# A hybrid streaming-encoder trunk: other ranks and places for weight sums, background loads, two norms and the first dots

## The chip, the cores and the metric

The kernel runs on one core of one Trainium2 chip. A core has five engines, each with its own instruction stream: TensorE (PE, matmuls; PEld is its weight load), VectorE (DVE), ScalarE (ACT), GpSimd (POOL) and SyncE (SP). An engine runs its instructions in the order in which they were put into its stream; it waits at an instruction until what that needs is there, and everything behind it waits too. Transfers are issued by SP, ACT and POOL and run on the core's DMA engines. The metric is the device time of one execution in microseconds (us), the median of several runs.

## The reference

Two layers over a sequence of 512 positions with 16 meta tokens ahead of it (T = 528), model width 2048. The even layer projects the normed input into a convolution group and an attention group, gates each, and projects the sum back; the odd layer is a gated linear recurrence with 16 heads.

```python
def even_mixer(hn, ...):
    glu_v, glu_g, gate_a, q, c, gate_b, qi, ki, wi = split_last(hn @ w_in, EVEN_SPLITS)
    u = glu_v * jax.nn.sigmoid(glu_g)
    u = conv(u, conv_w) + conv_b                       # causal, depthwise, width 31
    a_out = silu(layer_norm(u, ln_g, ln_b)) * silu(gate_a)
    c = rms_norm(c, kv_g)                              # the latent
    ...                                                # index dots, top-k mask, attention over c
    b_out = einsum(o_lat, w_uv) * silu(gate_b)
    return concatenate([a_out, b_out]) @ w_out

def odd_mixer(hn, ...):
    q, fz, i, g = split_last(hn @ w_in, ...)
    o = hgrn2_chunkwise(silu(q), log_f(fz), k(fz), i)
    o = rms_norm(o) * norm_g * silu(g)
    return o @ w_out

for layer in range(2):
    h = h + mixer[layer](rms_norm(h, norm_gain[layer]))
return rms_norm(h, final_norm_gain)[:, 16:]
```

## The kernel before

Everything lies transposed: features on the 128 partitions, positions along the free axis. A **stripe** (`stripe`) is 128 output features against all 2048 inputs. Its weights come as one 1 MB load `w`; `square_sum` (L192, ScalarE, output `junk`) adds up their squares, an all-reduce on POOL (L144, `tot`) sums over the partitions, and from that VectorE makes a power-of-two scale (`u` L148, `sc` L199, `inv` L201). Then each half is split into two float16 tiles: `wh` by ScalarE (L208) and `wl` by VectorE (L209). TensorE takes three matmuls for each k tile (wh by xh, wh by xl, wl by xh; L268 to L270), 96 for a stripe of two halves of 264 columns. `split` (L317, L318) makes the pairs xh and xl of the input in the same way.

The order of each engine's stream is made by a planner when the program is built: every instruction has a rank (`band`: WGT 5 above EVAC 4, SIDE 3, CONV 2), and the planner takes the ready one of the highest rank, by its own estimate of times. `behind(name)` puts what follows after the instruction that was noted as `queued[name]` on its stream. `at(us, job)` puts a side job behind a given point of a running count (`clock`) of the stripes' matmul time. The work runs in stages:

- **Input and first stripes.** x is loaded, normed and split into the 16 tiles X0 (L419, L317). Stripes `kw` and `c` come first; from `c` the latent is normed (`csq`, `rc`, L494). The bias table is built from `onehot` by four loads and small matmuls (L485) and written to DRAM (`bdram`).
- **EVEN stage.** A list gives the order of stripes: `g` convolution gates (`glu`, followed by 31 convolution steps on VectorE, L617 and L619, tile `z`), `s` index stripes (`scores`), `k` the top-k masks (`select`, L588 to L591), `h` attention heads (`head`, `attend`), `n` the layer norm. A `scores` stripe evacuates its two halves (L559, L560), exchanges them between partition halves by two transfers on POOL (L562, `uh<-pa` or `ul<-pa`), and its `dots` (L572, L573) follow as side jobs, 7 us later by the running count; ScalarE and VectorE add them into the masks (L575, L576). In a head, POOL loads a row block of biases (`L<-bdram`, L644), adds the mask to it by a transfer (`L<-mask`, L646), then come scores (L654), softmax (L656 to L663), transposes (L683, L686) and values (L697).
- **Background loads.** `later` holds 48 transfers on POOL's queue that form sums of output weights in DRAM (`es`, L368). `send` issues a few at a time: one or two at the places called `aside`, two in each `scores`, and one behind each mask of heads 6 and 7. `foresee` loads weights of later stages and squares them.
- **Layer norm** of the convolution, as two side jobs, `mean` and `spread` (Ln L335, Exp L336), rank CONV.
- **Mixing and first output.** Gates `gate_a`, then eight output **pairs** p, each of seven products of 24 matmuls (L979): `pair_begin` loads weights and, from p = 2, squares four of them; `pair_corner` and `pair_rest` do the products and the adds (`add`, L986). Within `pair_rest(0)` pair 2 is begun.
- **Odd layer.** 48 stripes and 16 recurrences (`rec_head`, L1150 to L1156 in its levels), then 16 gate stripes. Beside them the 16 weight blocks of the last output are loaded (`gw`) and squared, one in each gate stripe (two `junk` of 1024 columns), for `pair_scales`, which makes the scales of the last eight pairs. Then come these pairs (`pair_stripes`) and the final norm.

Of the kernel before, what the change touches and what calls it, by code (L numbers as in the profile page):

```python
# [74 lines left out]
def trunk_kernel(ctx: ExitStack, tc: tile.TileContext, x: bass.AP, w: bass.AP, wukv: bass.AP,  # L75
# [139 lines left out]
    def load(s, back, keep=None, known=None):  # L215

        w32 = load_raw(s)
        if known is None:
            ss = wpool.tile([128, 1], F32, name="ss", bufs=4)
            with behind("S"):  # L220
                square_sum(w32, ss)
            total = wpool.tile([128, 1], F32, name="tot", bufs=4) if keep is None else keep
            all_sum(total, ss)
            known = scales(total, back)
# [26 lines left out]
    def stripe(s, X, back, wide=True, order=(0, 1), ring=None, keep=None, known=None):  # L251
# [6 lines left out]
        with band(WGT):  # L258
            hi, lo, inv = load(s, back, keep, known)
# [54 lines left out]
    def split(pair, src, scale):  # L314

        xh, xl = pair[:, 0, :], pair[:, 1, :]
        S.activation(xh, src, AF.Identity, scale=scale)  # L317
# [98 lines left out]
    with band(WGT):  # L416
        for k in range(KT):
            t = et([128, T], F32, "sq", 3)
            V.tensor_tensor(t, xin[k], rstd0, op=OP.mult)  # L419
            X0.append(split(xp.tile([128, 2, T], F16, name="x", bufs=KT), t, gains[:, 0, k:k + 1]))  # L420

# [68 lines left out]
    with band(SIDE):  # L490
        rc = et([128, T], F32, "acc", 2)
        rstd_from(mean_bcast(ones_c, csq, None), rc, eps_r, et([128, T], F32, "sq", 3))
        for j in range(2):
            V.scalar_tensor_tensor(cn[j], cn[j], col(V_KV + j), rc, op0=OP.mult, op1=OP.mult)  # L494
            CX.append(split_rounded(E, cn[j]))
# [52 lines left out]
    def scores(j):  # L548
        ps, inv = stripe(S_QI + j, X0, back0, wide=False)
        catch_up()  # L550
        send(later, 2)
# [5 lines left out]
        with band(EVAC):  # L557
            for q, hi, lw, hf, other in ((qa, qa, ql, lo, up), (qb, ql, qb, up, lo)):
# [3 lines left out]
                G.dma_start(q[other], ql[hf])  # L562
# [16 lines left out]
        for t in range(NB):  # L579
            for hh in range(2):  # L580
                at(clock[0] + 7.0 + 1.2 * (2 * t + hh), lambda t=t, hh=hh: dots(t, hh))
# [17 lines left out]
    def glu(i):  # L599
        ps, inv = stripe(S_GLU + 2 * i, X0, half0)  # L600
        g = et([128, T], F32, "gt", 3)
        with band(EVAC):
            for p, sl in ps:
                S.activation(g[:, sl], p, AF.Tanh, scale=inv)
        aside(i > 2)
        ps, inv = stripe(S_GLU + 2 * i + 1, X0, back0)
        aside(i > 2)
# [29 lines left out]
    def attend(h, qh, gb, Kh, Vt):  # L637
# [4 lines left out]
        def softmax(t, nq, q0, W):  # L642
            e = et([128, T], F32, "L", 5)
            queued[f"B{h}"] = G.dma_start(e[:nq, :W], bias_rows(h, q0, nq, 0, W))  # L644
            if t < NB:
                queued["B"] = G.dma_start(e[:, :W], M[t], accum_op=OP.add)  # L646
                if h >= 6:
                    send(later, 1, "B")
# [69 lines left out]
    def head(h):  # L718
# [7 lines left out]
        aside(True)  # L726
        ps, inv = stripe(S_GQ + 2 * h + 1, X0, back0)
        catch_up()
        aside(True)
# [35 lines left out]
    def aside(late):  # L765

        send(later, 1 if late else 2)
# [5 lines left out]
    def layer_norm():  # L773

        def mean():
            with band(CONV):
# [5 lines left out]
                for p, sl in mean_bcast(ones_a, [zs], None):  # L782
                    S.activation(mu[:, sl], p, AF.Copy)
# [11 lines left out]
        def spread(vs_):  # L795
            nonlocal rz
            with band(CONV):
# [187 lines left out]
    def add(dst, p, scale):  # L985
        V.scalar_tensor_tensor(dst, p, scale, dst, op0=OP.mult, op1=OP.add)  # L986
# [63 lines left out]
    def pair_rest(p, raw, scale, banks, following):  # L1050
# [12 lines left out]
        for bank_, wt, xs, first, dst, scl in ((b, s2, u2, True, ha[:, t2], ninv), (a, w12, x21, False, ha[:, t1], inv),  # L1063
# [3 lines left out]
            with band(EVAC):  # L1067
                add(dst, bank_, scl)
                if wt is s4:
                    first_square(2 * p)  # L1070
# [299 lines left out]
    osc, oinv, oninv = oq[:, 2, :].bitcast(I32), oq[:, 3, :].bitcast(I32), oq[:, 4, :]  # L1370

    def pair_scales(c):

        sl = slice(4 * c, 4 * c + 4)
        with band(EVAC):
# [5 lines left out]
            V.tensor_scalar(osc[:, sl], u, -1.0, 204 * EXP, op0=OP.mult, op1=OP.add)  # L1381
            V.tensor_scalar(oinv[:, sl], u, oback, None, op0=OP.add)
            V.tensor_scalar(oninv[:, sl], oinv[:, sl].bitcast(F32), -1.0, None, op0=OP.mult)

    ahead = 1
    early_load(S_OO)
    for i in range(8):
        for h in (i, 8 + i):
# [20 lines left out]
    osc, oinv = osc.bitcast(F32), oinv.bitcast(F32)  # L1409
# [72 lines left out]
    for n in range(0, KT - 2, 2):  # L1482
        pair_stripes(n)
    with band(WGT):
# [127 lines left out]
```

## Time and profile before

| | us |
|---|---|
| median of 3 runs (lowest to highest) | 1842.26 (1841.38 to 1843.06) |
| the profiled execution | 1841.84 |
| its span in the trace | 1839.7 |
| VectorE busy | 1394.8 (76%) |
| ScalarE busy | 1237.3 (67%) |
| POOL busy | 225.3 (12%) |
| weight splits on ScalarE (`wh<-w,sc` L208) | 214 of 1143 ns |
| weight squares on ScalarE (`junk<-w` L192) | 114, mean 1674 ns |
| es loads on POOL's queue | 48 from the weights (512 KB, median 7.9 from issue to landing) and 16 from es |

How to read it: the page has one execution of the program. A row of a timeline gives the start, the duration, the engine, the line, the operation, out<-in with the shape, and in brackets how long the engine was idle before it and what ended that idle time. A row of the waits gives the waiting engine and line, the one waited for, us in total, how many times, and the longest. A row of the windows gives a stretch, its length, the busy time of each engine, the granted TensorE clock as a share of full speed, the DMA share and GB/s.

### The profile page before, as it was taken

Reading aid. Unit: us, or ns where it says so; the run is one execution under the profiler, and the core shown is the slowest. Engines: PE = TensorE matmul, PEld = TensorE weight load, DVE = VectorE, ACT = ScalarE, POOL = GpSimd, SP = SyncE. Lnnn points to the kernel's source line nnn. Section 1 sums busy time; section 2 is a strip of 40 time slices with the busy share of each in tenths; the row PEclk is TensorE's granted clock in tenths of the full one; section 3 lists DMA queues with packets and bytes.
Section 4 is the critical chain, followed back from the end, with each engine's and each line's share of the span. In section 5 each row is a group of like instructions: output and inputs, shape, how many; then the busy total and the mean of one; then the engine's idle time right before and its main releaser. Section 6 shows DMA issues by size and latency. Waiting matters only on the chain.

```text
span 1839.7 us, 36579 instructions
## 1 busy us (share of the span) xinstructions
PE 1802.2 (98%) x14678; PEld 1393.2 (76%) x14678; DVE 1394.8 (76%) x2836; ACT 1237.3 (67%) x2035; POOL 225.3 (12%) x399
## 2 busy tenths in 40 slices
PE   9989999999999899999999999999999999999997
PEld 6666588888888788888777777877777765446886
DVE  7599979998875577777787777777777776757774
ACT  4755675667666666675687777778787777865563
POOL 1312211132222200000110100101010000001000
PEclk9999999999999999999999999999999999999998
DMA  5856666668565745774665555455654445556553
GB/s 202 266 159 195 177 178 188 187 181 227 165 197 133 191 130 188 255 249 163 200 195 138 177 161 174 160 157 152 170 165 146 138 143 178 183 197 238 197 187 109
DMA packets 81339, 330.97 MB, mean 180 GB/s; under 512 B 10288, under 2 KB 17752, under 8 KB 65840
## 3 DMA queue, kind: packets, MB, share of 16 engines
q1 hardware_dynamic: 40592, 190.51, 29.4%
q0 software_dynamic: 25600, 87.64, 20.0%
q10 hardware_dynamic: 14976, 50.47, 8.3%
q8 instruction: 115, 1.88, 0.4%
q14 instruction: 56, 0.46, 0.1%
HBM read 309.75 MB, written 73.87 MB: 209 GB/s over the span
## 4 chain that ended last, share of the span: by engine, by line
PE 67%; DVE 6%; ACT 4%; issue 3%; DMA 2%; POOL 1%; ACTq 0%; SPq 0%; DVEq 0%; POOLq 0%
PE mps L268 15%; PE mps L269 15%; PE mps L270 15%; PE mps L979 13%; DVE z L619 2%; DMA w<-in_w_dram 1%; ACT junk L192 1%; DVE wl L209 1%; PE po L697 1%; PE s L979 1%; ACT wh L208 1%; PE s L1155 1%; PE s L1154 1%; PE s L1156 1%; PE po L1277 1%
## 5 line engine op out<-in xcount | busy, mean ns | idle before, releaser
L268 PE MATMUL mps<-x,wh 128*128 128x264 f16 (+1 forms) x2880 | 864.9, 300 | 2.8 <-ACT x L317 2.8
L270 PE MATMUL mps<-x,wl 128*128 128x264 f16 (+1 forms) x2880 | 864.6, 300 | 0.0
L269 PE MATMUL mps<-x,wh 128*128 128x264 f16 (+1 forms) x2880 | 864.3, 300 | 0.2
L268 PEld LDWEIGHTS <-wh 128*128 128x128 f16 x2880 | 283.1, 98 | 110.0 <-issue 7.9
L269 PEld LDWEIGHTS <-wh 128*128 128x128 f16 x2880 | 283.1, 98 | 108.0 <-issue 3.3
L270 PEld LDWEIGHTS <-wl 128*128 128x128 f16 x2880 | 283.0, 98 | 106.6 <-issue 2.9
L208 ACT ACTIVATE wh<-w,sc 128x1024 f16<-128x1024 f32 x214 | 243.3, 1143 | 136.3 <-PE mps L269 81.3
L209 DVE SCALAR_TENSOR_TENSOR wl<-w,sc,wh 128x1024 f16<-128x1024 f32 x214 | 272.6, 1279 | 57.5 <-ACT wh L208 55.9
L192 ACT ACTIVATE junk<-w 128x2048 bf16<-128x2048 f32 (+2 forms) x114 | 190.8, 1674 | 26.2 <-DMA w<-in_w_dram 23.3
L979 PEld LDWEIGHTS <-wh 128*128 128x128 f16 x1808 | 177.4, 98 | 28.6 <-issue 2.2
L619 DVE SCALAR_TENSOR_TENSOR z<-u,vec,z 128x528 f32<-128x528 f32 x240 | 179.4, 760 | 1.9
L144 POOL PARTITION_ALL_REDUCE tot<-ss x78 | 42.4, 543 | 688.2 <-ACT junk L192 688.2
L979 PEld LDWEIGHTS <-wl 128*128 128x128 f16 x904 | 88.7, 98 | 13.3 <-DVE wl L209 1.2
L208 ACT ACTIVATE wh<-w,oq 128x1024 f16<-128x1024 f32 x53 | 60.6, 1148 | 54.6 <-PE mps L979 46.3
L209 DVE SCALAR_TENSOR_TENSOR wl<-w,oq,wh 128x1024 f16<-128x1024 f32 x53 | 67.8, 1283 | 28.1 <-ACT wh L208 28.0
L979 PE MATMUL mps<-on,wh 128*128 128x256 f16 x464 | 78.1, 273 | 0.1
L192 ACT ACTIVATE junk<-gw 128x1024 bf16<-128x1024 f32 x64 | 66.9, 1045 | 2.5 <-DMA gw<-in_w_dram 2.2
L1151 DVE SCALAR_TENSOR_TENSOR qlm<-q,qhm 128x256 f16<-128x256 f32 x128 | 52.5, 421 | 20.8 <-ACT qhm L1150 20.8
L1150 ACT ACTIVATE qhm<-q 128x256 f16<-128x256 f32 x128 | 51.1, 411 | 21.7 <-DVE q L1252 19.3
L979 PE MATMUL mps<-on,wl 128*128 128x256 f16 x232 | 63.2, 273 | 0.0
L209 DVE SCALAR_TENSOR_TENSOR wl<-w,gsc,wh 128x1024 f16<-128x1024 f32 x32 | 41.0, 1281 | 28.4 <-ACT wh L208 28.2
L209 DVE SCALAR_TENSOR_TENSOR wl<-w,gaq,wh 128x1024 f16<-128x1024 f32 x30 | 38.5, 1283 | 22.3 <-ACT wh L208 22.1
(544 smaller groups left out, 3282.3 us busy)
## 6 DMA issues: line engine op xcount, KB each, us to landing
w<-in_w_dram SPq DMA_DIRECT2D x116, 1024.0 KB, 5.0
gw<-in_w_dram ACTq DMA_DIRECT2D x64, 512.0 KB, 6.4
es<-in_w_dram POOLq DMA_DIRECT2D x48, 512.0 KB, 7.9
w<-in_w_dram SPq DMA_DIRECT2D x47, 512.0 KB, 4.5
os<-in_w_dram POOLq DMA_DIRECT2D x42, 512.0 KB, 7.9
w<-es SPq DMA_DIRECT2D x32, 512.0 KB, 5.1
w<-os SPq DMA_DIRECT2D x28, 512.0 KB, 4.5
pa<-in_w_dram ACTq DMA_DIRECT2D x24, 512.0 KB, 4.0
```

Of the source, the lines that this page charges most:

```text
L144: queued["G"] = G.partition_all_reduce(out, src, channels=128, reduce_op=op or bass_isa.ReduceOp.add)
L192: S.activation(junk[:, :src.shape[-1]], src, AF.Square, accum_out=ss)
L208: queued["S"] = S.activation(hi, src, AF.Identity, scale=sc)
L209: V.scalar_tensor_tensor(lo, src, sc, hi, op0=OP.mult, op1=OP.subtract)
L268: P.matmul(o, hi[half][:, ws], xh[:, sl], start=n == 0 and k == 0, stop=False)
L269: P.matmul(o, hi[half][:, ws], xl[:, sl], start=False, stop=False)
L270: mm = P.matmul(o, lo[half][:, ws], xh[:, sl], start=False, stop=n == 1 and k == 7)
L619: V.scalar_tensor_tensor(z, u[:, j:j + T], col(V_CW + i * CW + j), z, op0=OP.mult, op1=OP.add)
L697: P.matmul(state["o"][:, 128 * t:128 * (t + 1)], Vt[:, j, :], pt[:, j, :], start=j == 0, stop=j == t + 1)
L979: P.matmul(p, wt[:, sl], xt, start=start and k == i == 0, stop=stop and k == 7 and i == 2, skip_group_check=stop and not start and resume)
L1150: S.activation(hi, src, AF.Copy, scale=scale)
L1151: V.scalar_tensor_tensor(lo, src, scale, hi, op0=OP.mult, op1=OP.subtract)
```

## The change

It moves work and leaves what is computed as it was.

- The square sum of the first index stripe's weights is put behind the split of the last input tile (`early="X0"`).
- The latent norm becomes a side job at 6.0 of the running count, of rank EVAC, with one table of functions loaded behind the first convolution gate's tanh.
- The dots of the first index stripe come 14 instead of 7 us later; no background load is sent in that stripe, and in the others they are sent behind the exchange. The first convolution gate sends none, the others two at each `aside`, the heads one, the masks of heads 6 and 7 none.
- The layer norm's mean matmuls, their evacuation and the Ln and Exp get rank EVAC.
- Pair 2 is begun in `pair_rest(1)`, so that on ScalarE all splits of pair 1 stand ahead of the four square sums of pair 2; the weights of the stripe behind the last pair, or of any stripe behind a noted `V`, come behind the add of the last `s4`.
- Gate stripes 0 and 8 do no weight squares; the last two blocks are squared behind the first two pairs of the last output.

```diff
@@ load, stripe, split
-    def load(s, back, keep=None, known=None):
+    def load(s, back, keep=None, known=None, early="S"):
...
-            with behind("S"):
+            with behind("S"), behind(early):
                 square_sum(w32, ss)
...
-        with band(WGT):
-            hi, lo, inv = load(s, back, keep, known)
+        with band(WGT), behind("V"):
+            hi, lo, inv = load(s, back, keep, known, early)
+        queued.pop("V", None)
...
-        S.activation(xh, src, AF.Identity, scale=scale)
+        queued["A"] = S.activation(xh, src, AF.Identity, scale=scale)
...
             X0.append(split(xp.tile([128, 2, T], F16, name="x", bufs=KT), t, gains[:, 0, k:k + 1]))
+        queued["X0"] = queued["A"]
@@ the latent norm
-    with band(SIDE):
-        rc = et([128, T], F32, "acc", 2)
-        rstd_from(mean_bcast(ones_c, csq, None), rc, eps_r, et([128, T], F32, "sq", 3))
...
+    def latent():
+        with band(EVAC):
+            rc = et([128, T], F32, "acc", 2)
+            pieces = mean_bcast(ones_c, csq, None)
+            with behind("T"):
+                ready = S.preload_act_table_set("natural_log_exp_and_others")
+            with tc.issue_after(ready.ins):
+                rstd_from(pieces, rc, eps_r, et([128, T], F32, "sq", 3))
...
+    at(6.0, latent)
@@ scores
-        ps, inv = stripe(S_QI + j, X0, back0, wide=False)
+        ps, inv = stripe(S_QI + j, X0, back0, wide=False, early="X0" if j == 0 else "S")
         catch_up()
-        send(later, 2)
...
-                G.dma_start(q[other], ql[hf])
+                queued["X"] = G.dma_start(q[other], ql[hf])
+        if j:
+            send(later, 2, "X")
...
-                at(clock[0] + 7.0 + 1.2 * (2 * t + hh), lambda t=t, hh=hh: dots(t, hh))
+                at(clock[0] + (7.0 if j else 14.0) + 1.2 * (2 * t + hh), lambda t=t, hh=hh: dots(t, hh))
@@ glu, softmax, head, aside
-                S.activation(g[:, sl], p, AF.Tanh, scale=inv)
-        aside(i > 2)
+                queued["T"] = S.activation(g[:, sl], p, AF.Tanh, scale=inv)
+        aside(2 if i else 0, i > 2)
...
                 queued["B"] = G.dma_start(e[:, :W], M[t], accum_op=OP.add)
-                if h >= 6:
-                    send(later, 1, "B")
...
-        aside(True)
+        aside(1, True)
...
-    def aside(late):
+    def aside(n, late):
 
-        send(later, 1 if late else 2)
+        send(later, n)
         if late:
             foresee()
@@ layer_norm
-                for p, sl in mean_bcast(ones_a, [zs], None):
-                    S.activation(mu[:, sl], p, AF.Copy)
+                with band(EVAC):
+                    for p, sl in mean_bcast(ones_a, [zs], None):
+                        S.activation(mu[:, sl], p, AF.Copy)
...
         def spread(vs_):
             nonlocal rz
-            with band(CONV):
+            with band(EVAC):
@@ pair_rest
-                add(dst, bank_, scl)
+                last = add(dst, bank_, scl)
                 if wt is s4:
+                    queued["V"] = last
                     first_square(2 * p)
...
-        nxt = pair_rest(p, *begun[p], banks[p], p + 2 if p == 0 else p + 1 if p > 1 else 8)
+        nxt = pair_rest(p, *begun[p], banks[p], p + 1 if p else 8)
@@ the gates and the last output
-    ahead = 1
+    ahead = 0
+
+    def early_square():
+
+        nonlocal ahead
+        for c in range(2):
+            square_sum(raws.pop(0), oss[:, ahead, c:c + 1])
+        ahead += 1
+        if ahead < KT:
+            early_load(S_OO + ahead)
+        if ahead % 8 == 0:
+            pair_scales(ahead // 16)
+
...
             with band(CONV), behind("S"):
-                if raws:
-                    for c in range(2):
-                        square_sum(raws.pop(0), oss[:, ahead - 1, c:c + 1])
-                if ahead < KT:
-                    early_load(S_OO + ahead)
-                ahead += 1
-            if ahead in (9, 17):
-                pair_scales(ahead // 16)
+                if h not in (0, 8) or i:
+                    early_square()
...
         pair_stripes(n)
+        if ahead < KT:
+            with band(CONV), behind("S"):
+                early_square()
```

Line numbers of the changed kernel are one higher from L268 on, and about 10 to 13 higher from L494 on. Three places in the streams:

On ScalarE, in the first stripes, before (`junk,ss` are square sums, `x<-sq,gains` the input tiles):

```order
L469 ACTIVATE sq<-gb 128x528
L208 ACTIVATE wh<-w_743,sc 128x1024 x2
L469 ACTIVATE sq<-gb 128x528
L192 ACTIVATE junk,ss<-w_901 128x2048
L317 ACTIVATE x<-sq,gains 128x528
L208 ACTIVATE wh<-w_901,sc 128x1024 x2
```

and now:

```order
L471 ACTIVATE sq<-gb 128x528
L208 ACTIVATE wh<-w_742,sc 128x1024 x2
L471 ACTIVATE sq<-gb 128x528
L318 ACTIVATE x<-sq,gains 128x528
L192 ACTIVATE junk,ss<-w_898 128x2048
L208 ACTIVATE wh<-w_898,sc 128x1024 x2
```

The last `x` (L317, now L318) stands ahead of the square sum of the next stripe's weights.

On POOL, between the bias table and the first exchange (`uh<-pa`), before (`ISA tot` is an all-reduce):

```order
L144 ISA tot<-ss 128x1
L368 DMA es_189<-in_w_dram 128x1024
L368 DMA es_191<-in_w_dram 128x1024
L487 DMA bdram<-z 128x1x352
L644 DMA L<-bdram 128x1x528
L644 DMA L<-bdram 16x1x16
L144 ISA tot<-ss 128x1
L368 DMA es_193<-in_w_dram 128x1024
L368 DMA es_184<-in_w_dram 128x1024
L562 DMA uh<-pa 64x512 x2
```

and now:

```order
L656 DMA L<-bdram 128x1x528
L656 DMA L<-bdram 16x1x16
L144 ISA tot<-ss 128x1
L369 DMA es_183<-in_w_dram 128x1024
L369 DMA es_185<-in_w_dram 128x1024
L144 ISA tot<-ss 128x1
L572 DMA uh<-pa 64x512 x2
L144 ISA tot<-ss 128x1
L369 DMA es_184<-es_183 16x8192
```

The two es loads right ahead of the exchange (before: `uh<-pa` in the last row, now in the last but two) gave way to an all-reduce, and the last bias loads moved up ahead of another all-reduce. Ahead of the whole piece eight es loads stood and two stand.

In POOL's stream at the last head, before:

```order
L646 DMA L<-mask_603 128x144
L368 DMA es_206<-in_w_dram 128x1024
L644 DMA L<-bdram 16x1x16
L646 DMA L<-mask_606 128x272
L368 DMA es_210<-es_208 16x8192
L646 DMA L<-mask_609 128x400
L368 DMA es_212<-in_w_dram 128x1024
L646 DMA L<-mask_612 128x528
L852 DMA u<-mbd 128x528
```

and now:

```order
L658 DMA L<-mask_573 128x144
L656 DMA L<-bdram 16x1x16
L658 DMA L<-mask_576 128x272
L658 DMA L<-mask_579 128x400
L658 DMA L<-mask_582 128x528
L863 DMA u<-mbd 128x528 x2
L863 DMA kih<-mbd 128x528
```

No es load stands between the masks any more.

More of the change, by code (lines that the diff above doesn't have):

```diff
@@ L249, in columns, with stripe @@
         return (slice(0, HT), slice(HT, T)) if wide else (slice(NM, T),)
-    def stripe(s, X, back, wide=True, order=(0, 1), ring=None, keep=None, known=None):
+    def stripe(s, X, back, wide=True, order=(0, 1), ring=None, keep=None, known=None, early="S"):
         catch_up()
@@ L489, in trunk_kernel @@
     CX = []
-    with band(SIDE):
-        rc = et([128, T], F32, "acc", 2)
-        rstd_from(mean_bcast(ones_c, csq, None), rc, eps_r, et([128, T], F32, "sq", 3))
-        for j in range(2):
-            V.scalar_tensor_tensor(cn[j], cn[j], col(V_KV + j), rc, op0=OP.mult, op1=OP.mult)
-            CX.append(split_rounded(E, cn[j]))
+    def latent():
[6 more added lines that the diff above has]
+                rstd_from(pieces, rc, eps_r, et([128, T], F32, "sq", 3))
+        with band(SIDE):
+            for j in range(2):
+                V.scalar_tensor_tensor(cn[j], cn[j], col(V_KV + j), rc, op0=OP.mult, op1=OP.mult)
+                CX.append(split_rounded(E, cn[j]))
+    at(6.0, latent)
     blocks = [(0, NM)] + [(NM + 128 * b, 128) for b in range(NB)]
@@ L603, in glu @@
             for p, sl in ps:
-                S.activation(g[:, sl], p, AF.Tanh, scale=inv)
-        aside(i > 2)
+                queued["T"] = S.activation(g[:, sl], p, AF.Tanh, scale=inv)
+        aside(2 if i else 0, i > 2)
         ps, inv = stripe(S_GLU + 2 * i + 1, X0, back0)
-        aside(i > 2)
+        aside(2 if i else 0, i > 2)
         v = et([128, T], F32, "gt", 3)
@@ L725, in head @@
         gb = gate(S_GQ + 2 * h, "gb", stat[:, 1, h:h + 1])
-        aside(True)
+        aside(1, True)
         ps, inv = stripe(S_GQ + 2 * h + 1, X0, back0)
         catch_up()
-        aside(True)
+        aside(1, True)
         qh = et([128, T], F32, "qh", 2)
@@ L985, in add @@
     def add(dst, p, scale):
-        V.scalar_tensor_tensor(dst, p, scale, dst, op0=OP.mult, op1=OP.add)
+        return V.scalar_tensor_tensor(dst, p, scale, dst, op0=OP.mult, op1=OP.add)
     def first_square(n):
@@ L1369, in trunk_kernel @@
     oq = ht([128, 5, 8], F32, "oq")
-    osc, oinv, oninv = oq[:, 2, :].bitcast(I32), oq[:, 3, :].bitcast(I32), oq[:, 4, :]
+    osci, oinvi, oninv = oq[:, 2, :].bitcast(I32), oq[:, 3, :].bitcast(I32), oq[:, 4, :]
+    osc, oinv = oq[:, 2, :], oq[:, 3, :]
     def pair_scales(c):
@@ L1380, in pair_scales @@
             half_exponent(u, oq[:, 1, sl])
-            V.tensor_scalar(osc[:, sl], u, -1.0, 204 * EXP, op0=OP.mult, op1=OP.add)
-            V.tensor_scalar(oinv[:, sl], u, oback, None, op0=OP.add)
-            V.tensor_scalar(oninv[:, sl], oinv[:, sl].bitcast(F32), -1.0, None, op0=OP.mult)
-    ahead = 1
+            V.tensor_scalar(osci[:, sl], u, -1.0, 204 * EXP, op0=OP.mult, op1=OP.add)
+            V.tensor_scalar(oinvi[:, sl], u, oback, None, op0=OP.add)
+            V.tensor_scalar(oninv[:, sl], oinv[:, sl], -1.0, None, op0=OP.mult)
+    ahead = 0
[8 more added lines that the diff above has]
+            pair_scales(ahead // 16)
     early_load(S_OO)
@@ L1399, in trunk_kernel @@
             with band(CONV), behind("S"):
-                if raws:
-                    for c in range(2):
-                        square_sum(raws.pop(0), oss[:, ahead - 1, c:c + 1])
-                if ahead < KT:
-                    early_load(S_OO + ahead)
-                ahead += 1
-            if ahead in (9, 17):
-                pair_scales(ahead // 16)
+                if h not in (0, 8) or i:
+                    early_square()
         group(i)
-    osc, oinv = osc.bitcast(F32), oinv.bitcast(F32)
     acc2 = ht([128, SEQ], F32, "sg", 2)
```

## The prediction

> **What bounds the kernel.** I began with the page's busy shares.
>
> ```profile
> PE 1802.2 (98%) x14678; PEld 1393.2 (76%) x14678; DVE 1394.8 (76%) x2836; ACT 1237.3 (67%) x2035; POOL 225.3 (12%) x399
> ```
>
> TensorE is busy for 98% of the 1839.7 us span and the change takes no weight matmul away. So the time can only fall where TensorE waits, or where it is granted less than its full clock. The waits of engine PE come next: who was waited for, us in total, times, longest.
>
> ```profile
> PE s L572 <- DMA uh<-pa: 4.9, 1, 4.9
> PE s L654 <- DVE st L656: 3.7, 2, 3.6
> PE mps L268 <- ACT x L317: 2.8, 1, 2.8
> PE s L1154 <- ACT qhm L1150: 2.3, 2, 2.1
> PE mps L979 <- DVE h L986: 1.6, 1, 1.6
> PE s L979 <- ACT wh L208: 1.5, 1, 1.5
> PE s L654 <- ACT acc L335: 1.2, 1, 1.2
> PE po L697 <- ACT pt L687: 1.1, 1, 1.1
> PE s L979 <- DVE wl L209: 0.9, 1, 0.9
> PE s L686 <- ACT acc L335: 0.9, 1, 0.9
> ```
>
> These are few and single: 21 us in ten rows, 1.1% of the span. Then the stretches around them (us from the span's start; length; busy PE, PEld, DVE, ACT, POOL; then the granted clock, DMA share and GB/s):
>
> ```profile
> 60.00:70.00 10.00, 7.16 (x57) 5.36 (x55) 4.31 (x8) 5.62 (x7) 1.85 (x4) 0.93 1.03 353
> 70.00:80.00 10.00, 10.00 (x64) 7.07 (x63) 3.87 (x6) 6.09 (x8) 2.28 (x4) 0.72 0.96 328
> 100.00:112.00 12.00, 7.05 (x64) 5.93 (x61) 11.83 (x18) 5.92 (x7) 2.31 (x5) 0.90 0.77 197
> 112.00:120.00 8.00, 8.00 (x50) 6.33 (x51) 5.90 (x13) 3.20 (x7) 1.25 (x2) 0.72 0.86 262
> 260.00:320.00 60.00, 60.00 (x531) 52.82 (x531) 58.31 (x168) 37.13 (x62) 7.45 (x14) 1.00 0.62 190
> 642.00:652.00 10.00, 9.23 (x53) 7.16 (x54) 7.23 (x19) 7.28 (x18) 1.23 (x2) 0.66 0.73 178
> 734.00:742.00 8.00, 7.97 (x56) 6.31 (x57) 5.41 (x14) 2.30 (x2) 1.48 (x3) 0.79 0.44 164
> 868.00:880.00 12.00, 10.36 (x79) 8.75 (x78) 4.92 (x9) 4.78 (x6) 1.33 (x3) 1.00 0.59 197
> 1536.00:1544.00 8.00, 8.00 (x51) 3.65 (x49) 7.20 (x15) 4.71 (x10) 0.00 (x0) 0.79 0.35 143
> ```
>
> A second loss shows: behind a wait of 2.1 us or more the clock is granted at less than 1.00 for a while, behind the 1.6 us of the stretch from 868 it is not. I price it as (1 - clock) x length: 0.7 + 2.8 = 3.5 us behind the wait for x, 1.2 + 2.2 = 3.4 behind the exchange, 3.4 at 642, 1.7 at 734, 1.7 at 1536. The undisturbed stretch from 260 gives two more sizes: 60 us hold 531 matmuls, 0.113 us each, and VectorE is busy for 58.3 of them.
>
> [...]
>
> **The change, place by place.**
>
> *Place A, the last x.* ScalarE (times: start, duration):
>
> ```profile
> 65.60 1.91 ACT L192 ACTIVATE junk<-w 128x2048 bf16<-128x2048 f32 x1 [4.11 <-DMA w<-in_w_dram]
> 67.51 0.72 ACT L317 ACTIVATE x<-sq,gains 128x528 f16<-128x528 f32 x1
> ```
>
> The last x stood behind a square sum that itself waited 4.11 us for its weights, and TensorE waited 2.8 us. Now `behind("X0")` puts that square sum after x, which can start where the square sum began to wait, at 65.60 - 4.11 = 61.5. Gain 2.8 + 3.5 = 6.3. What is late next: the third bias matmul moves up to half a microsecond after this place, and its onehot DMA stands on POOL's queue behind the all-reduce of that same square sum. Bounds 0 to 6 us (a whole new wait with its clock loss); the competing es loads are gone from the queue, so I take 0.5.
>
> *Place B, the exchange of s0's halves.*
>
> ```profile
> 103.39 1.15 ACT L208 ACTIVATE wh<-w,sc 128x1024 f16<-128x1024 f32 x1 [5.16 <-DVE sc L199]
> 108.44 0.51 POOL L562 DMA_DIRECT2D uh<-pa  x1 [0.17 <-issue]
> 111.93 0.55 PE L572 MATMUL s<-kih,uh 128*128 128x256 f32 x1 [4.95 <-DMA uh<-pa]
> ```
>
> The exchange was issued late, because the ScalarE split before it stood behind a weight split that waited 5.16 us for its scale; its second half then needed 111.93 - 108.44 = 3.5 us to land. The first dots now stand 52 matmuls (5.9 us) later in TensorE's order, and four es loads instead of twelve are sent ahead of that exchange. 4.9 + 3.4 = 8.3. The five bias loads and one more all-reduce now stand ahead of it on POOL; if they hold it, the old wait is back (bounds 0 to 8.3). I take 0.5.
>
> The latent norm's Ln and Exp come to share a table: two table loads fewer on ScalarE, 1.28 us each by the row under C. No wait of TensorE above lies there, its stripes run beside them, so I cost it at nothing; without that cover it is 2.6 us of gain.
>
> *Place C, the layer norm (595 to 602).*
>
> ```profile
> 596.45 1.28 ACT L336 ACT_TABLE_LOAD   x1
> ```
>
> This is one of four loads, by which Ln and Exp of two halves alternate; TensorE's waits there sum to 1.2 + 1.1 + 0.9 = 3.2. The higher rank moves Ln up, but the four loads stay, and two attention splits now stand between them. Bounds: 3.2 gained, 3.4 lost (a wait that grows past 2.1 and costs the clock of 642). I take nothing, since the same four loads remain.
>
> *Place D, head 7's masks.*
>
> ```profile
> 632.65 1.24 POOL L646 DMA_DIRECT2D L<-mask  x1
> 633.23 1.55 POOL L368 DMA_DIRECT2D es<-in_w_dram  x1
> 633.78 1.91 POOL L646 DMA_DIRECT2D L<-mask  x1
> 642.13 0.57 DVE L656 CUSTOM_DVE_ANT_0 L<-s,L 128x400 f32<-128x400 f32 x1 [5.46 <-DMA L<-mask]
> ```
>
> A mask took 9.5 us from issue (632.65) to use, with es loads between its neighbours. All es loads are now sent before head 6's bias loads. 3.6 + 3.4 = 7.0 gained; the tile loads behind them follow closer, so I leave 0.5 (bounds 0 and the 7.0).
>
> *Place F, pair 1's weights.*
>
> ```profile
> 730.47 1.06 ACT L192 ACTIVATE junk<-w 128x1024 bf16<-128x1024 f32 x1 [1.44 <-DMA w<-in_w_dram]
> 731.52 1.13 ACT L208 ACTIVATE wh<-w,gaq 128x1024 f16<-128x1024 f32 x1
> ```
>
> A square sum for pair 2 waited 1.44 us for its load and then ran, ahead of the split that TensorE wanted. Pair 2 now begins within pair 1's rest; the four square sums stand behind all the splits. 1.5 + 0.9 + 1.7 = 4.1. Next late are pair 2's own weights, whose sums start later: bounds 0 to 4.1, I take 0.5.
>
> *Place G, 872.*
>
> ```profile
> 871.63 2.48 DVE L209 SCALAR_TENSOR_TENSOR wl<-w,sc,wh 128x1024 f16<-128x1024 f32 x2 [1.16 <-ACT wh L208]
> 874.02 0.89 DVE L986 SCALAR_TENSOR_TENSOR h<-mps,inv,h 128x264 f32<-128x264 f32 x2
> ```
>
> Two weight splits of the next stripe stood before the adds that free PSUM; `behind("V")` turns that round: 1.6. What is late now are those splits, by the 0.9 us of the adds; bounds 0 and 0.9, and as no wait above lies at that stripe's start I take nothing.
>
> *Place H, the first gates.*
>
> ```profile
> 1532.14 1.04 ACT L192 ACTIVATE junk<-gw 128x1024 bf16<-128x1024 f32 x1
> 1533.74 0.42 ACT L1150 ACTIVATE qhm<-q 128x256 f16<-128x256 f32 x1 [0.47 <-PE s L1156]
> ```
>
> ScalarE has no idle time here, and heads 0 and 8 no longer do square sums: four of 1.04, and their four load issues, go to the gates after them and to the first two output pairs, whose scales are wanted two pairs later. 2.1 + 1.7 = 3.8. If that slack were gone, the four cost 4.2 at the end.
>
> *What is late next for all of it.* The first head's last mask:
>
> ```profile
> 239.18 0.97 DVE L576 SCALAR_TENSOR_TENSOR mask<-sq,wiT,mask 128x264 f32<-128x264 f32 x2 [2.65 <-ACT sq L575]
> 354.68 0.90 POOL L646 DMA_DIRECT2D L<-mask  x1 [0.36 <-DVE mask L591]
> 368.18 0.73 ACT L663 ACTIVATE L<-L,st 128x528 f32<-128x528 f32 x1 [1.07 <-DVE st L662]
> 369.82 0.60 PE L683 MATMUL s<-ident,L 128*128 128x128 f32 x4
> ```
>
> The stretch from 260 shows VectorE as good as without idle time on its way to the mask. The softmax ends at 368.9, and TensorE takes it at 369.8: 0.9 us to spare. TensorE now arrives 14.6 us earlier (A and B), and 14 matmuls (1.6 us) earlier in its own order. VectorE starts its convolution only as much earlier as A gives (6.3) and can win the rest only out of its idle time before 239, such as the 2.65. Bounds: nothing, if it keeps pace; at worst 14.6 - 6.3 + 0.7 = 9.0, and 3.4 of clock. I take 2.0, nearer to keeping pace, because at 239 VectorE was waiting for TensorE's dots and not the reverse.
>
> **The sum.** Gains 6.3 + 8.3 + 7.0 + 4.1 + 1.6 + 3.8 = 31.1; new waits 0.5 + 0.5 + 0.5 + 0.5 + 2.0 = 4.0; net 27.1. The profiled execution took 1841.84 us (2.14 around its span), 0.42 below the median of 1842.26. 1842.26 - 27.1 = 1815.2; I say 1815.
>
> **Rivals.**
>
> 1. *VectorE takes the start back.* The first head's mask comes late by most of the 9.0, and the clock falls behind it: say 7, so 1815 - 2.0 + 7 + 3.4 = 1823. For it: VectorE busy for 58.3 of 60 us, and 0.9 us of slack. Against: its wait at 239. Chance 0.22.
> 2. *It does not do what it says at B and D.* POOL still holds the exchange behind the bias loads, and head 7's masks still land after 9 us, beside the h loads: 15.3 is not gained, 1815 + 15.3 = 1830. For it: the mask's landing without es loads is not in the row. Against: 3.5 us for the exchange even beside es loads. Chance 0.13.
> 3. [...]
> 4. *Slower: the es loads meet every exchange.* They are sent two at a time behind each convolution gate and each exchange, where they were also sent in the heads. If an exchange then takes longer than the 5.9 us that B's dots gain, the dots of the seven later stripes wait like B's, 4.9 + 3.4 = 8.3 each. It turns slower from four such stripes on (33 against 27); five would give 1815 + 41.5 = 1856. Against: 3.5 us was measured with es loads in flight. Chance 0.06.
>
> **How the numbers follow.** Forecast 0.50; rivals 0.22, 0.13, 0.05, 0.06; 0.04 for several small returns that end near no change. 0.2% is 3.7 us, about what a measurement of this kernel can tell from no change: faster 0.88, same 0.05, slower 0.07. The range starts at 1805, where no new wait appears, C's 3.2 goes and a few rows under 1 us with it (1842.3 - 31.1 - 3.2 = 1808), and reaches 1834, past rival 2.
>
> **What would show it.** In the profile after: no wait of PE on x L318, on uh or on st above 1 us; no clock below 0.99 at 70, 112, 640, 735 and 1537; pair 1's splits in one row without a square sum between. A wait of L693 for ScalarE near 355 with a lowered clock behind it is rival 1. The forecast is wrong if the dots of s0 still wait, or if new waits of over 2 us appear in the convolution stage.

## The result, and the profile after

| | before | changed |
|---|---|---|
| median of 4 runs each (lowest to highest), us | 1842.66 (1841.38 to 1845.10) | 1822.47 (1822.24 to 1824.37) |
| the profiled execution, us | 1841.84 | 1822.30 |
| its span, us | 1839.7 | 1820.5 |
| mean granted clock | 0.990 | 0.998 |

The ratio is 0.9891 [0.9874, 0.9908]: 20 us faster, where 27 were forecast. In the profiled executions it is 19.5. The busy shares and the longest waits of TensorE in the changed kernel:

```profile
PE 1790.4 (98%) x14678; PEld 1388.1 (76%) x14678; DVE 1393.0 (77%) x2836; ACT 1232.0 (68%) x2033; POOL 227.2 (12%) x399
...
PE s L584 <- ACT sq L587: 4.2, 3, 1.7
PE s L1166 <- ACT qhm L1162: 2.5, 2, 2.2
PE s L693 <- ACT L L673: 1.9, 1, 1.9
...
PE s L664 <- ACT acc L336: 1.7, 1, 1.7
PE po L707 <- ACT pt L697: 1.4, 3, 0.8
PE mps L270 <- DVE x L319: 1.2, 1, 1.2
```

TensorE does the same 14678 matmuls in 11.8 us less of busy time (1802.2 to 1790.4). Its idle time falls from 37.5 to 30.1 (span less busy), so by 7.4. So more than half of the gain in these two profiles is clock, not waiting: a matmul at a lowered clock counts as busy, only longer (from 734 to 742 the same 8 us of busy time held 56 matmuls at 0.79 and hold 74 at 1.00). The windows show where (length; busy PE, PEld, DVE, ACT, POOL; clock, DMA share, GB/s). The first six are places that the prediction speaks of (a wait for `qhm`, place H, now ends at 1509.6), the last two the index stage:

```profile
60.00:70.00 10.00, 10.00 (x83) 7.51 (x80) 6.97 (x12) 9.09 (x12) 1.26 (x4) 1.00 0.66 246
70.00:80.00 10.00, 10.00 (x80) 8.42 (x80) 5.00 (x11) 9.71 (x16) 3.04 (x6) 1.00 0.87 243
112.00:120.00 8.00, 8.00 (x57) 5.75 (x56) 8.00 (x17) 5.23 (x13) 1.46 (x2) 1.00 0.53 200
642.00:652.00 10.00, 10.00 (x89) 8.75 (x88) 8.55 (x17) 6.87 (x12) 0.57 (x1) 1.00 0.39 134
734.00:742.00 8.00, 8.00 (x74) 6.95 (x72) 6.77 (x12) 6.41 (x7) 1.48 (x3) 1.00 0.75 256
1510.00:1520.00 10.00, 9.81 (x87) 5.07 (x85) 9.76 (x24) 6.73 (x15) 0.00 (x0) 1.00 0.30 94
...
220.00:240.00 20.00, 18.30 (x137) 14.06 (x136) 10.60 (x23) 10.93 (x23) 5.00 (x8) 1.00 0.98 253
240.00:260.00 20.00, 17.50 (x148) 14.57 (x147) 16.38 (x52) 15.00 (x29) 3.14 (x6) 1.00 0.77 195
```

The stretches that had 0.66 to 0.79 before are at 1.00, and so is the last gates', and where TensorE had been idle it is busy throughout: the waits of A, B, D and F are gone. New is the index stage, in which TensorE now stands still for 1.7 + 2.5 us. The kernel before has no idle time from 220 to 260; the first half of that:

```profile
220.00:240.00 20.00, 20.00 (x108) 11.44 (x107) 15.27 (x29) 11.19 (x22) 2.95 (x4) 1.00 0.55 151
```

The DMA share (the last but one number) went from 0.55 to 0.98. The timeline of the changed kernel at two of its three new waits there, and at one that a later head got:

```profile
232.99 1.06 ACT L192 ACTIVATE junk<-pa 128x1024 bf16<-128x1024 f32 x1 [3.42 <-DMA pa<-in_w_dram]
234.04 0.48 ACT L587 ACTIVATE sq<-s 128x400 f32<-128x400 f32 x1
234.58 0.39 PE L584 MATMUL s<-kih,uh 128*128 128x264 f32 x1 [1.71 <-ACT sq L587]
241.71 0.33 SPq L513 DMA_DIRECT2D w<-in_wukv_dram  x1
248.15 1.06 ACT L516 ACTIVATE uh<-w 128x1024 fp32r<-128x1024 f32 x1 [3.07 <-DMA w<-in_wukv_dram]
249.65 0.39 PE L584 MATMUL s<-kih,ul 128*128 128x264 f32 x1 [1.72 <-ACT sq L587]
...
404.56 1.81 POOL L658 DMA_DIRECT2D L<-mask  x2 [6.68 <-DMA L<-bdram]
407.86 0.31 DVE L666 CUSTOM_DVE_ANT_0 L<-s,L 128x144 f32<-128x144 f32 x1 [3.82 <-DMA L<-mask]
412.04 0.33 PE L693 MATMUL s<-ident,L 128*128 128x128 f32 x1 [1.92 <-ACT L L673]
```

At 232.99 ScalarE does a square sum after 3.42 us of waiting for its load. Behind it in the stream stands the `sq` that TensorE's dots need. The dots that it reads were done at 230.8, so it is ready and can't pass. At 248.15 the same happens with the first split of `wukv`. In each case the row of the waits names ScalarE; ScalarE itself was idle 3 us, waiting for a transfer. At 407 VectorE was idle too: the mask came late through POOL.

### The profile page after: what moved, and what is told of

The parts are those of the page before. It is cut to its first block, busy times and chain, and to the rows that moved or that the text cites. A ratio compares the mean times of both kernels' runs of the same rounds, so it can differ in the third digit from the quotient of the medians.

```text
span 1820.5 us, 36572 instructions
## 1 busy us (share of the span) xinstructions
PE 1790.4 (98%) x14678; PEld 1388.1 (76%) x14678; DVE 1393.0 (77%) x2836; ACT 1232.0 (68%) x2033; POOL 227.2 (12%) x399
## 4 chain that ended last, share of the span: by engine, by line
PE 82%; DVE 8%; issue 3%; ACT 2%; DMA 2%; POOL 1%; SPq 0%; ACTq 0%; DVEq 0%; POOLq 0%
PE mps L271 18%; PE mps L270 18%; PE mps L269 18%; PE mps L990 15%; DVE mask L601 2%; DVE wl L209 2%; DVE m L600 1%; PE s L291 1%; PE s L990 1%; PE mps L291 1%; DVE z L631 1%; PE po L707 1%; PE po L1289 1%; PE s L1167 1%; PE s L1168 1%
## 5 line engine op out<-in xcount | busy, mean ns | idle before, releaser
L1162 ACT ACTIVATE kt1h<-k 128x256 f16<-128x256 f32 x64 | 26.5, 414 | 41.5 <-DVE k L1255 27.7
```

The lines of the kernel that those rows point to most:

```text
L1162: S.activation(hi, src, AF.Copy, scale=scale)
```

## The experiments

Two theories stood at first. **Theory one:** the seven missing microseconds lie in crowded transfers: the es loads, taken out of the first stripes and the last heads' masks, are now bunched between 180 and 250. The rival: they lie with the engines, VectorE's load or the order that the change's other edits give (squares at the gates, the add at 872). Kernels of one submission share a chip and the runs of before, whose medians were 1842.16, 1843.32 and 1842.65. Unless said otherwise, the edits below are edits to the changed kernel. All ratios are to the kernel before.

### es_old: the old places of the es loads from the index stage on

```diff
-            send(later, 2, "X")
+            send(later, 2)
...
-        aside(2 if i else 0, i > 2)
+        aside(1 if i > 2 else 2 if i else 0, i > 2)
...
                 queued["B"] = G.dma_start(e[:, :W], M[t], accum_op=OP.add)
+                if h >= 6:
+                    send(later, 1, "B")
```

> The changed kernel with the old schedule of the background es loads behind the first index stripe: two right after each further index stripe, one at each place of the gates from the fourth on, one behind each mask of heads 6 and 7; all the rest as changed. Changed kernel: 1822.5 us, TensorE waits 4.2 us for the index dots' ScalarE (sq L587) and the DMA share is 0.98 from 220 to 240. Theory 1, crowded transfers (es loads bunched between 180 and 250 make a weight load on ScalarE's queue late, and ScalarE stands still in front of the dots): the wait for sq falls below 1.0 us and the DMA share there below 0.80; head 7's masks come late again with their lowered clock (+7): 1822.5 - 4 + 7 = about 1825. Theory 2, TensorE merely arrives earlier than ScalarE and VectorE can follow: the wait for sq stays above 3 us, about 1829.

1826.38, ratio 0.9915 [0.9888, 0.9943]. No wait for `sq` is left, and `wukv` is used 4.3 us after its issue instead of 6.4; the DMA share was 0.56 from 220 to 240 and 0.61 from 240 to 260, instead of 0.98 and 0.77. But D came back (waits, window, timeline):

```profile
PE s L666 <- DVE st L668: 4.9, 1, 4.9
...
628.00:640.00 12.00, 9.56 (x57) 7.41 (x58) 7.07 (x20) 7.61 (x19) 1.35 (x2) 0.72 0.90 228
...
244.22 1.06 ACT L516 ACTIVATE uh<-w 128x1024 fp32r<-128x1024 f32 x1 [0.91 <-DMA w<-in_wukv_dram]
```

Both halves of the mechanism show: es loads among head 7's masks cost 4.9 us and a clock of 0.72; the same loads in the index stage cost the `sq` waits. Their number is fixed, so the edit trades one place for the other.

### es_thin: one load instead of two behind each exchange, two instead of one in the heads

```diff
-            send(later, 2, "X")
+            send(later, 1, "X")
...
-        aside(1, True)
+        aside(2, True)
```

> The changed kernel with one es load instead of two in each index stripe, and two instead of one at the first place of each head, so that as many are sent in all and none later than head 7. Theory 1, crowded transfers: wait for sq L587 from 4.2 to below 1.5 us, DMA share from 220 to 240 from 0.98 to below 0.85, time 1818 to 1820. Theory 2, TensorE merely arrives earlier: wait for sq stays above 3 us, time 1821 to 1824; two loads per head may cost at the masks.

1828.03, 0.9921 [0.9893, 0.9950]. The wait for `sq` fell from 4.2 to 1.5, as theory one has it, but its time of 1818 to 1820 was missed: the loss came out at the heads (waits and a window):

```profile
PE s L693 <- ACT L L673: 5.8, 2, 3.9
...
445.00:452.00 7.00, 6.79 (x35) 4.80 (x36) 5.85 (x19) 3.71 (x9) 0.00 (x0) 0.63 0.70 109
```

### sq_old and sq_late: the squares of the last output's weights

The first edit undoes place H, the second goes further: no squares in the first two gates of both groups, and two blocks behind each of the first output pairs.

```diff
-                if h not in (0, 8) or i:
-                    early_square()
+                early_square() if ahead < KT else None
```

```diff
-                if h not in (0, 8) or i:
+                if i > 1:
...
-        if ahead < KT:
-            with band(CONV), behind("S"):
-                early_square()
+        for _ in range(2):
+            if ahead < KT:
+                with band(CONV), behind("S"):
+                    early_square()
```

> The changed kernel with the squares of the last output's weights back in all gate stripes, the first two included. Theory of the prediction, ScalarE's square sums ahead of the recurrence's splits set the wait there (2.5 us for qhm L1162 in the changed kernel): the wait grows by about 2.1 us to 4.6, with a lowered clock behind it: 1825 to 1827. Rival, the table loads and the chain over VectorE set it and the square sums fill gaps: the wait stays between 2 and 3 us, time 1821.5 to 1823.5.

> The changed kernel with no such squares in the first four gate stripes either (four more square sums move to the first two pairs of the last output, two blocks at each). Theory of the prediction: the wait for qhm falls from 2.5 to below 0.5 us, time 1819.5 to 1820.5. Rival, table loads and the chain over VectorE: the wait stays above 1.5 us, time 1821.5 to 1823.5, or more if the output pairs then wait for their scales.

sq_old: 1824.82 (1820.14 to 1832.57), 0.9904 [0.9866, 0.9942]. The waits for `qhm` were 2.3, against 2.5 in the changed kernel: putting all the squares back did not make them grow. But they are not the same waits. In sq_old, as in the kernel before, the long one (2.11 and 2.12 us) is at a matmul on `kt0h`; in the changed kernel it is at one on `kt1h`, 2.22 us, ending at 1509.61. Before (first two rows) and changed (last row):

```profile
1534.37 1.13 ACT L208 ACTIVATE wh<-w,gsc 128x1024 f16<-128x1024 f32 x1
1535.86 0.19 PE L1154 MATMUL s<-qhm,kt0h 128*128 128x64 f16 x1 [2.12 <-ACT qhm L1150]
...
1501.62 1.04 ACT L192 ACTIVATE junk<-gw 128x1024 bf16<-128x1024 f32 x1
```

sq_late: 1822.31, 0.9885 [0.9860, 0.9911], and the wait fell to 0.3. So in the changed kernel ScalarE's squares do stand in front of the `qhm` that TensorE wants; what stood there in the kernel before is taken up below, at H. The time of sq_late hides that gain, for its profile has 6.6 us of waits for `sq` instead of 4.2, with the same program up to there (waits and timeline):

```profile
PE s L584 <- ACT sq L587: 6.6, 3, 5.3
...
240.49 0.33 SPq L513 DMA_DIRECT2D w<-in_wukv_dram  x1
250.51 1.06 ACT L516 ACTIVATE uh<-w 128x1024 fp32r<-128x1024 f32 x1 [6.65 <-DMA w<-in_wukv_dram]
```

This load of 512 KB was used 10.0 us after its issue, against 6.4 in the changed kernel. sq_old's profile, from its slowest run, has 7.1 us of such waits. Both disagree with an explanation by order alone: what differs is how long the transfer took. The DMA share from 220 to 240 was 0.98 in the changed kernel and 1.01 in sq_late, from 240 to 260 it was 0.77 and 0.66, so the share alone does not tell it.

### kv_behind and kv_es: the split of wukv out of the way, then fewer es loads

kv_behind is sq_late with the load and the split of `wukv` put behind the latest tanh of a convolution gate, so that this split no longer stands ahead of the dots' `sq`. kv_es also sends one es load behind each exchange and three, three and two at the convolution gates; it leaves out one of the 64 es transfers, the last, so it does not compute the whole result.

```diff
     def keys_values(pr):
-        with band(WGT):
+        with band(WGT), behind("T"):
```

```diff
-            send(later, 2, "X")
+            send(later, 1, "X")
...
-        aside(2 if i else 0, i > 2)
+        aside((0, 3, 3, 2)[min(i, 3)], i > 2)
```

> sq_late, and besides the keys' weights of a head pair (wukv) are loaded and split behind the last convolution gate's tanh, so that on ScalarE this split no longer stands in front of the last index dots. In sq_late TensorE waited 6.6 us for sq L587, 5.3 of it at 246. Theory, ScalarE stands still there for that load: the wait for sq falls to 2 us or less, time 1822.3 - 5 = 1816.5 to 1818. Rival, any other transfer in the crowd takes its place, or the later load holds up weights: the waits in the convolution stage stay above 4 us, time 1820.5 or more.

> kv_behind, with one es load instead of two in each index stripe and three instead of two at each place of the second and third convolution gates, so that fewer are under way from 180 to 250. Theory of crowded transfers: DMA share from 220 to 240 from about 1.0 to below 0.85, what is left of the wait for sq below 1 us, time 1 to 2 us below kv_behind. Rival, the earlier loads meet the exchanges of the first index stripes: a wait for uh or ul above 2 us, time at or above kv_behind.

kv_behind: **1816.34** (1815.48 to 1818.86), 0.9858 [0.9836, 0.9880]. Its slowest run is 3 us below the fastest of the changed kernel's eight. Its waits:

```profile
PE s L584 <- ACT sq L587: 1.0, 1, 1.0
PE s L1166 <- ACT qhm L1162: 0.3, 1, 0.3
```

One place in ScalarE's order takes the wait for `sq` from 6.6 (sq_late) to 1.0, below every profile with the old place and the same es loads (3.3 to 7.1). The load of `wukv` still goes out at 241.35, as in the changed kernel (241.71); only its split moved, from its place at 248 to one behind the tanh. The transfers are still crowded (DMA share 0.83 between 240 and 260), but the dots' `sq` no longer stands behind this one. kv_es: 1812.28, 0.9840 [0.9815, 0.9865], without any wait for `sq` or on L673; it sends 47 of the 48 transfers from the weights and the 16 from es, and the run best below shows how much hangs on the missing one.

### add_old: VectorE's splits again ahead of the last adds

```diff
                 if wt is s4:
-                    queued["V"] = last
                     first_square(2 * p)
```

> The changed kernel without the note that puts the next stripe's weights behind the add of the last s4. Theory of the prediction: the wait for h L997 returns with 1.6 us and nothing else moves: 1824. Rival, the wait for the last x (L319, 1.2 us, with 0.5 beside it, at 892) is the same loss in its next place and goes when the splits are earlier: one wait for the other, time 1822 to 1823.

1833.64 (6 runs), 0.9950 [0.9931, 0.9970]. The wait at 872 did not come back. A larger one came 20 us later, at the odd layer's input (waits of TensorE, timeline of ScalarE, a window):

```profile
PE mps L270 <- DVE x L319: 5.6, 4, 2.9
...
877.55 1.91 ACT L192 ACTIVATE junk<-w 128x2048 bf16<-128x2048 f32 x1 [5.13 <-DMA w<-in_w_dram]
879.46 0.83 ACT L336 ACTIVATE rstd<-s,eps_r 128x264 f32<-128x264 f32 x2
...
902.00:909.00 7.00, 6.79 (x25) 3.27 (x25) 5.29 (x15) 2.61 (x6) 4.08 (x7) 0.56 0.90 307
```

Here is what the note does on ScalarE. In add_old a square sum (877.55) waits 5.13 us for its weights, and behind it in the stream stands the `rstd` of the odd layer's norm (879.46). With the note, the changed kernel has that `rstd` ahead of the square sum:

```profile
866.83 0.83 ACT L336 ACTIVATE rstd<-s,eps_r 128x264 f32<-128x264 f32 x2
...
878.17 1.91 ACT L192 ACTIVATE junk<-w 128x2048 bf16<-128x2048 f32 x1 [0.16 <-DMA w<-in_w_dram]
```

The norm is 12.6 us earlier by it. Without it the input tiles are late by 5.6 us of waits in place of 1.2, and (1 - 0.56) x 7 = 3.1 us of clock follow. Neither theory had this; it is the index stage's mechanism again, a late load with wanted work behind it on ScalarE.

### x_old, x_alone, es_start: what made the last x late

x_old takes back the order at place A (`early="S"` for the first index stripe). x_alone is the kernel before with that order alone. es_start is the kernel before without the es loads of the first convolution gate and the first index stripe:

```diff
         catch_up()
-        send(later, 2)
+        if j:
+            send(later, 2)
...
-        aside(i > 2)
+        aside(i > 2, i)
...
-        send(later, 1 if late else 2)
+        send(later, 0 if i == 0 else 1 if late else 2)
```

> The changed kernel with the first index stripe's square sum ahead of the last x again. Theory of the prediction, the places add up: the wait for x (2.8) and a lowered clock (3.5) return, 1828 to 1829.5. Rival, what the start gains is given back later: TensorE then arrives later in the convolution stage, the waits there (sq L587 4.2, L673 1.9) shrink by 2 us or more, and the time is 1824 to 1826.5.

> The kernel before with one edit alone: the first index stripe's square sum goes behind the last x. Theory of the prediction (the order on ScalarE set the wait): the wait for x L317 (2.8) and the lowered clock behind it (3.5) go, about 1836 against 1842.5. Rival after x_old (the es loads made that weight load late; without them the order does not matter, with them the order alone must still help): both edits suffice, each by itself, so also about 1836; if the wait at 65 stays above 1.5 us, the order was not the cause.

> The kernel before with one edit alone: no es loads in the first convolution gate and the first index stripe. Theory of the prediction: the wait for x stays (its order is as before), only part of the wait for the exchange uh goes: 1837 to 1842. Rival after x_old: the weight load lands sooner, ScalarE no longer stands still before x, and the wait for x (2.8) and its clock loss (3.5) go without any change of order: 1833 to 1837.

x_old: 1824.98, 0.9901 [0.9876, 0.9926]; x is at 64.19 behind the square sum, which did not wait, and TensorE does not wait for it. x_alone: 1842.68 (10 runs), 0.9996 [0.9984, 1.0008]; nothing gained, where both theories had 1836. es_start: 1837.44 (6 runs), 0.9974 [0.9959, 0.9990]; this lies between the two theories' times, and other waits move in it too, so the profiles decide. ScalarE and the stretch from 70 in x_alone:

```profile
61.97 0.72 ACT L317 ACTIVATE x<-sq,gains 128x528 f16<-128x528 f32 x1
66.32 1.91 ACT L192 ACTIVATE junk<-w 128x2048 bf16<-128x2048 f32 x1 [3.63 <-DMA w<-in_w_dram]
...
70.00:80.00 10.00, 7.67 (x43) 4.93 (x42) 4.19 (x6) 8.14 (x11) 3.19 (x6) 0.80 0.98 338
```

and in es_start:

```profile
61.60 1.89 ACT L192 ACTIVATE junk<-w 128x2048 bf16<-128x2048 f32 x1
64.02 0.72 ACT L317 ACTIVATE x<-sq,gains 128x528 f16<-128x528 f32 x1
...
70.00:80.00 10.00, 10.00 (x78) 8.19 (x77) 1.78 (x2) 9.84 (x15) 2.13 (x5) 1.00 0.86 239
```

With the new order alone, x is early, but the weights still land late (66.3). TensorE then waits 1.0 us for the onehot load, which the prediction had named as next late, and between 70 and 80 another 2.3 for a gate's evacuation (`gt`), and its clock is 0.80 from 70 to 80. With the old order and no es loads the weights are there at 61.6, and nothing waits. So at place A the es loads taken out gave the gain: without them the order is not needed (x_old, es_start), and with them it does not help (x_alone).

### best and changed_again

best is kv_es with the missing transfer sent at the last gate of the mixing (`send(later, 1 if i < 7 else len(later))`); changed_again is the changed kernel beside it.

> kv_es with all 64 es transfers sent (the one that was not goes behind the last gate of the mixing stage). Theory of crowded transfers, as for kv_es: no wait for sq above 1 us, no wait for L673 in the second head, 1812 to 1814. Rival: kv_es was faster for the transfer that it left out, or by the luck of its clock: 1815 to 1817, as kv_behind.

> The changed kernel once more beside the last one, on the same chip. 1822.5 us before. If the waits at 246 and 448 vary from run to run as in sq_late and sq_old (1.9 to 6.2 us, nothing to 3.8 us, in instructions that are alike up to there), its times spread over 5 us or more and its profile shows a wait for sq other than 4.2 us; if those were effects of the other edits, it shows 4.2 again and times within 2 us.

best: 1820.49, 0.9883 [0.9866, 0.9899]; changed_again: 1825.25 (1823.89 to 1826.49), 0.9905 [0.9890, 0.9920]. The changed kernel's times lie 2.6 us apart here, but its profile has other waits than the first: 3.3 us for `sq` (2.5 of them in one, with a clock of 0.93 from 220 to 240) and 2.3 for a head's `qh`. best is 8 us behind kv_es for one transfer. The planner put it ahead of a head's bias loads. POOL in kv_es:

```profile
560.36 0.52 POOL L369 DMA_DIRECT2D es<-es  x1 [1.69 <-DMA es<-in_w_dram]
560.86 1.11 POOL L656 DMA_DIRECT2D L<-bdram  x2
```

and in best, with what waited for it:

```profile
563.81 0.52 POOL L369 DMA_DIRECT2D es<-es  x1 [1.67 <-DMA es<-in_w_dram]
569.91 0.81 POOL L369 DMA_DIRECT2D es<-in_w_dram  x1 [5.58 <-DMA es<-es]
570.45 2.43 POOL L656 DMA_DIRECT2D L<-bdram  x4
...
584.32 0.31 DVE L666 CUSTOM_DVE_ANT_0 L<-s,L 128x144 f32<-128x144 f32 x1 [8.51 <-DMA L<-mask]
586.96 0.47 PE L693 MATMUL s<-ident,L 128*128 128x128 f32 x1 [6.47 <-ACT L L673]
```

POOL stood 5.6 us at the one transfer, which adds to the sum that the es transfer before it writes and waits until that has landed. The biases behind it went out at 570 instead of 561, and TensorE waited 6.5 us for the softmax, with a clock of 0.66 from 580 to 590. So kv_es's 1812 is not to be had by sending that transfer there; kv_behind is the fastest complete version that ran.

## Why the prediction was right, and where its sizes were off

The direction was right, and the time, 1822 against 1815, lies inside the range. The terms are right in part for other reasons than the prediction's. The sum by its own terms, with the profiled execution of the changed kernel:

| term | forecast | profile after |
|---|---|---|
| A, last x | 6.3 | 6.3: no wait, clock 1.00 |
| B, exchange of s0's halves | 8.3 | 8.3: likewise |
| C, layer norm | 0 | 0.7: waits 1.2 + 1.1 + 0.9 before, 1.7 + 0.8 now |
| D, head 7's masks | 7.0 | 7.0: no wait for `st`, clock 1.00 |
| F, pair 1's weights | 4.1 | 4.1 |
| G, adds at 872 | 1.6 | 0.4: gone, but TensorE waits 1.2 for x L319 at 894 |
| H, first gates | 3.8 | 1.5: clock 1.7, the waits 2.3 before and 2.5 now |
| new waits | -4.0 | -7.9: TensorE idle 4.2 from 220 to 260, 1.0 from 355 to 366 (first head), 2.4 from 405 to 420 (second head), 0.3 from 626 to 656 (head 7) |
| sum | 27.1 | 20.4; the spans differ by 19.2 |

The 1.2 us between the sum and the spans lies in small waits elsewhere and in the prices of the clock: (1 - clock) x length gives 13.7 for A, B, D, F and H, and the busy time fell by 11.8.

- **A had the right size and the wrong cause.** The prediction put the gain down to the square sum being moved behind x, and counted the missing es loads only as a reason for a small residual. x_old, x_alone and es_start show the reverse. The size came out because the change holds both edits; the one that the prediction credits gains nothing alone.
- **B, D and F** went as written. es_old brought D back by its own mechanism, the es loads between the masks. For B, es_start kept the 7 us distance of the dots and had six es loads ahead of the exchange (twelve before, four in the changed kernel), and still waited 3.1 us for `uh`. So fewer loads alone did not remove the wait; whether the later dots alone would was not tried.
- **"What is late next for all of it" is the term that was mis-sized:** 4.0 forecast (0.5 at each of A, B, D and F, and 2.0 at the first head's last mask), 7.9 measured, 0.3 of it at D and none at A, B or F. The first head cost 1.0 of its 2.0, but for `qh` (0.6) and `pt` (0.3), not for the softmax behind its last mask, so rival 1 did not come. Missing was the index stage, and with it the second head. The prediction looked at VectorE, which had no slack from 260 on (busy for 58.3 of 60 us); VectorE was idle at these waits, for 3.7 us up to 234.6, 3.0 up to 249.6 and 3.8 up to 407.9. What was late were transfers, with ScalarE or POOL standing in order in front of them. Rival 4 had the right transfers (es loads beside the index stripes) but let them delay the exchange, 8.3 us a stripe; instead they delayed other loads on other queues, at three dots. The DMA share of the stretch, 0.55 in the row of before, was where to look: 18 es transfers go out between 180 and 250 now, and 7 did before.
- **H** had the wrong instruction in front. Its own row shows ScalarE idle for 0.47 us behind the square sum of 1532.14, waiting for TensorE, so "no idle time" was a misreading and that sum did not set the wait. TensorE began to wait at 1533.7; from there ScalarE did a `qhm`, a `kt0h` and a weight split of 1.13 us (1534.37), and the `qhm` that TensorE wanted stood behind these. In the changed kernel that wait is gone, and one of the same size came at `kt1h`. There ScalarE has no idle time from 1489 on, and two square sums (the second at 1501.62) and two table loads lie on its way. sq_late, which takes those sums out too, removed 2.2 of 2.5 us. So the change gained nothing in waits here, and its 1.7 of clock is luck, as the last section shows.
- **G:** 1.6 was exchanged for 1.2 at 894, yet add_old shows that without this edit the changed kernel loses 5.6 - 1.2 + 3.1 = 7.5 us there. The prediction priced an edit by the wait that it removes in the kernel before; in the changed one it prevents another.
- **The clock:** at A and F the losses, 5.2 us by the prediction's prices, went with their waits, which speaks for the waits as their cause. At H the loss went though a wait of 2.2 us stands there, so that one decides nothing. The prediction's sign of being wrong, a new wait of over 2 us in the convolution stage, was just missed in this profile (1.9 at the longest) and appears in changed_again (2.5), with a clock of 0.93 from 220 to 240 and of 0.76 from 1513 to 1520. Before its last 15 us no stretch of 5 us in the first profile has a lowered clock, so its mean of 0.998 is a good draw (0.995 to 0.997 in the other three runs).

What stays open: by how much the index stage's waits differ from run to run. Four profiles of the same program up to there (changed, changed_again, sq_old, sq_late) have 4.2, 3.3, 7.1 and 6.6 us for `sq`, and the times of sq_old lie 12 us apart.

## What to carry to other kernels

In the complete versions that ran, background transfers could be moved but not made free: TensorE waited 4.2 us for `sq` with them bunched in the index stage, and 4.9 us at head 7 with them among its masks (es_old). Wherever they are bunched, look at each engine whose next instruction needs a load, and ask what that is ready stands behind it in the same stream. Moving the waiting instruction behind what TensorE wants (kv_behind: 6.6 to 1.0 us) did more here than moving the transfers, which in es_old and es_thin only chose who was to wait. A term that prices a removed wait should be checked against the changed kernel's schedule, not only that of before (add_old), and a gain that two edits could bring needs each tried alone (x_alone, es_start).

## What the runs showed of the hardware

Equal waits did not cost equal clock. Two profiles of the same program, the changed kernel's and changed_again, have the same wait of 2.2 us for `qhm` at the same matmul. In the first the clock stayed at 1.00 (the row of 1510 above). In changed_again it was 0.76 over the 7 us from that matmul on:

```profile
1513.04 0.19 PE L1166 MATMUL s<-qhm,kt1h 128*128 128x64 f16 x1 [2.22 <-ACT qhm L1162]
...
1513.00:1520.00 7.00, 6.78 (x44) 3.44 (x44) 6.97 (x15) 4.53 (x10) 0.00 (x0) 0.76 0.01 2
```

That is (1 - 0.76) x 7 = 1.7 us more for the same wait. A wait of 3.1 us for `uh` in es_start cost no clock (1.00 from 98 to 120), waits of up to 2.9 for x in add_old did (0.56). So the loss behind a wait of 2 to 3 us is a matter of chance as far as these runs tell, and the prediction's limit of 2.1 us, with its certain loss, was too neat.

Also unexpected was how far a load's landing varies: ScalarE stood waiting for the one of `wukv` and used it 4.3 (es_old), 6.4 (changed) and 10.0 us (sq_late) after its issue, at almost the same point of the program (issues at 239.93, 241.71 and 240.49) and with a DMA share of 0.61, 0.77 and 0.66 from 240 to 260.
